# First channel mixer of a hybrid decoder trunk: from plain up projections to 17 folded pairs, and 32 modulation columns moved into the mLSTM heads

## The chip, the cores and the metric

The kernel runs on one core of a Trainium2 chip. The metric is the device time of one execution in microseconds (us). Times are medians of several executions; beside them stands one execution that was recorded by the hardware profiler, and every row of a profile comes from that one.

## What is computed

The trunk has two layers on a residual stream of 512 tokens by 1024 channels in float32. Layer 0 has a retention mixer, layer 1 an mLSTM mixer, and each layer then has a channel mixer (ConvFFN). Every mixer gets a normalised input, scaled and shifted by modulations that come from a vector c, and a third modulation (a gate) multiplies its output. Cut to what matters:

```python
def conv_ffn(h, w_up, conv_w, conv_b, w_down):
    u = causal_dwconv(h @ w_up, conv_w, conv_b)      # 1024 -> 2 x 2816, then 3 taps along the tokens
    a, b = jnp.split(u, 2, axis=-1)
    return (jax.nn.silu(a) * b) @ w_down             # 2816 -> 1024

c_act = jax.nn.silu(c)
for i in range(DEPTH):
    mod = c_act @ ada_w[i] + ada_b[i]
    sh_t, sc_t, gt_t, sh_f, sc_f, gt_f = [m[:, None, :] for m in jnp.split(mod, 6, axis=-1)]
    h = rmsnorm(x, norm_tok_g[i]) * (1.0 + sc_t) + sh_t
    y = retention_mixer(h, ...) if i % 2 == 0 else mlstm_mixer(h, ...)
    x = x + gt_t * y
    h = rmsnorm(x, norm_ffn_g[i]) * (1.0 + sc_f) + sh_f
    x = x + gt_f * conv_ffn(h, ffn_w_up[i], ffn_conv_w[i], ffn_conv_b[i], ffn_w_down[i])
return rmsnorm(x, final_g)
```

## The kernel before

**Layout.** Channels lie on the 128 partitions, tokens along the free axis: x is eight tiles of 128x512. A float32 product is made of three TensorE matmuls of parts of lower precision, high by high, high by low and low by high (`mm3`, L250 to L253). So each operand has a high and a low part, "hh" and "hl" for an input, "whi" and "wlo" for weights, "ggh" and "ggl" for the gated product that goes into the down projection.

**Weights** come in chunks of 512 KB (`Chunk`, L172): a load on the queue of SP into a raw buffer (a pool of eight, `RAWS`, which weights, modulation rows and the folding's buffers share), the high part as a cast on ScalarE (L157), the low part as a subtraction on VectorE (L162), into pools of eight (`WBUFS`).

**Modulations.** One column of 128 modulations is one instruction on VectorE over 128x1025 elements, with a sum (`gemv`, L134), on a row block `ada` of 512 KB that SP loads. Sixteen are taken at the very start; the other 80 stand in a list `side` (gates of layer 0's token mixer, 8; layer 0's channel mixer, 24; layer 1's token mixer, 24; layer 1's channel mixer, 24).

**Order of the work.** The kernel first builds a list `items`: each has the weight chunks that it uses, a function, and a flag `free`. A loop (from L1363) goes through them: it issues loads, high and low parts of chunks up to a few items ahead, though not past an item in `bars`, then calls the function, and then, behind an item that uses weights, is free and is not among the first, takes one entry off `side`. A scheduler then settles the order of each engine's instructions, by costs; inside a folded mixer's `run` the order is as written for TensorE, VectorE, ScalarE and GpSimd.

**The stages**: setup, retention heads, channel mixer 0, mLSTM heads, channel mixer 1, last normalisation. `heads` (L827) sets the order within the two token mixers: q and k, v, scores ("w", "sp", "sh", "sl": L1280 to L1284), gate, attention ("pav", "pden") of the four heads, with one head's parts between the next head's projections.

**Between stages** stand `boundary` (L580) and `Start`. `boundary` does the last contraction in two halves of the columns; under the second half the squares of the first are summed, its root is taken and normalised inputs are made. `Start` runs the first four projections of the next stage side by side ("pf" tiles), first for one half of the columns and then for the other, while the rest of the normalisation ends. With `folded=True` it keeps the normalised input "xr" too, and makes sums of it (`sums` and `turn`) which the folded products need, on VectorE, GpSimd and ScalarE.

**Channel mixer** (`Ffn`, L866). There are 22 pairs of up projections (one row block of the "a" half, one of the "b" half) and 22 row blocks of the down projection, in groups (`GROUPS`).
- Mixer 0 is *plain*. Each up projection ("pp" tiles, `proj_item`) is 24 matmuls of 512 columns; the convolution (L879, L884), silu, product and split follow on ScalarE and VectorE. The groups are 6, 8 and 8: the first two are contracted between projections ("po" tiles), the last in the boundary.
- Mixer 1 is *folded* from pair 5 on (`FOLD_FROM`). Pairs 0 and 1 are in `Start`, pairs 2 to 4 are six plain projections. Each of the other 17 pairs is a unit of `folded` (L374): instead of the eight half-size products of two projections it does seven products of combined weights and combined inputs, 12 matmuls of 256 columns each ("p" tiles, L387 to L389), and in between two pieces of the down projection, 12 matmuls of 512 columns each. `Fold` (L183) makes the combined weights of a pair from its two chunks "wa" and "wb": sums "ws" (L213, L214) and "wt" (L219, L220) on VectorE, high parts on ScalarE, low parts as a negated copy on ScalarE with an adding DMA on GpSimd's queue behind it (L165 to L170), or by a subtraction on VectorE. Unit 0's weights are prepared under the six plain projections, those of each later unit inside the unit before. The groups are 4, 4, 4, 4 and 6.

Of the kernel before, what the change touches and what calls it, by code (L numbers as in the profile page):

```python
# [22 lines left out]
FF = 2816  # L23
FT = FF // P
EPS = 1e-6
GROUPS = [[6, 8, 8], [4, 4, 4, 4, 6]]
WCOLS = 1024
WBUFS = 8
RAWS = 8
FOLD_FROM = 5  # L30
WPAD = 64
OFF = 16
# [37 lines left out]
def trunk(ctx: ExitStack, tc: tile.TileContext, xT, cb, pos, vec, decay, zmask, ada, w_s0, w_in0, w_v0,  # L70
# [4 lines left out]
    wpool = ctx.enter_context(tc.tile_pool(name="wpool", bufs=WBUFS))  # L75
    raws = ctx.enter_context(tc.tile_pool(name="raws", bufs=RAWS))
    cols = ctx.enter_context(tc.tile_pool(name="cols", bufs=4))
# [17 lines left out]
    def bank(s):  # L95
        return psum.tile([P, T], F32, tag="ps", name=uid(s))
# [75 lines left out]
    class Chunk:  # L172
        def __init__(self, src, n, off):
            self.raw, self.r, self.off = wide(uid("raw")), slice(0, n), off
            nc.sync.dma_start(self.raw[:, self.r], src)
# [74 lines left out]
    def mm3(o, ah, al, bh, bl, start, stop):  # L250
        PE.matmul(o, ah, bh, start=start, stop=False)  # L251
        PE.matmul(o, ah, bl, start=False, stop=False)  # L252
        PE.matmul(o, al, bh, start=False, stop=stop)  # L253
# [61 lines left out]
    items = []  # L315
# [7 lines left out]
    def item(uses, fn, free=True):  # L323
        for u in uses:
            if u.first is None:
                u.first = len(items)
            u.last = len(items)
        items.append((uses, fn, free))

    bars = []  # L330
    class Ahead:
# [5 lines left out]
        @property  # L337
        def flat(self):
            if not hasattr(self, "all"):
                self.all = [u for n, (uses, _, _) in enumerate(items) for u in uses if u.first == n]  # L340
            return self.all
# [19 lines left out]
    ahead = Ahead()  # L361

    side = []

    def proj_item(src, h, then):
        def fn(w):
            ps = bank("pp")
            for k in range(KT):
                cs = slice(k * P, k * P + P)
                mm3(ps[:], w[0].hi[:, cs], w[0].lo[:, cs], h[k].hi[:], h[k].lo[:], k == 0, k == KT - 1)  # L370
            then(ps)
        item([Use(src, KT * P)], fn)

    def folded(folds, h, terms, pairs, downs, ahead):  # L374
# [31 lines left out]
        def unit(i):  # L406
# [47 lines left out]
            if with_down:  # L454
                down(i, 0)
            else:
                product(i, 5, c1[:, HB])
# [9 lines left out]
            if d:  # L467
                d.high()
                d.low()
            down(i, 1)  # L470
            if f:
                f.high_b()
# [79 lines left out]
    def contract_tiles(w, n, gate, ys, i, t0, t1, after=lambda m: None, js=None):  # L552

        r = slice(t0, t1)
        per = WCOLS // (n * P)
        for j in js or range(per):
            m = i * per + j
            ps = bank("po")
            for k in range(n):
                cs = slice((j * n + k) * P, (j * n + k) * P + P)  # L560
                mm3(ps[:, r], w.hi[:, cs], w.lo[:, cs], ys(k).hi[:, r], ys(k).lo[:, r], k == 0, k == n - 1)
            add_residual(ps, m, gate(m), t0, t1)
            after(m)

    def pieces(src, n, gate, ys):

        per = WCOLS // (n * P)

        def piece(i):
            def run(w, t0, t1, after=lambda m: None, js=None):  # L570
                contract_tiles(w, n, gate, ys, i, t0, t1, after, js)
            return Use(src(i), per * n * P), run
        return [piece(i) for i in range(KT // per)]

    def contract_items(ps, between=lambda i: None):
        for i, (u, run) in enumerate(ps):
            item([u], lambda w, run=run: run(w[0], 0, T))
            between(i)

    def boundary(late, last, norm):  # L580


        for u, _ in late + last:
            u.off = OFF
        for p, after in ((0, lambda m: norm.square(0, m)), (1, norm.later)):
            for u, run in late:
                item([u], lambda w, run=run, p=p: run(w[0], *HALVES[p]), False)
                if p:
                    norm.beside()
            for u, run in last:  # L590
                item([u], lambda w, run=run, p=p, after=after: run(w[0], *HALVES[p], after), False)
        norm.rest()
# [268 lines left out]
    def gate_col(layer, which):  # L861
        base = (16, 40)[which]
        return lambda m: mods[layer][:, base + m : base + m + 1]


    class Ffn:  # L866
        def __init__(self, layer):
            self.layer, self.h, self.gs = layer, [], {}
            t0, t1 = self.pair(0), self.pair(1)
            w = w_up[layer]  # L870
            self.folded = layer == 1
            self.start = Start([w[0], w[FT], w[1], w[FT + 1]], self.h, layer, 1, [t0, t0, t1, t1], self.folded)

        def conv_col(self, f, j):
            return col("fcw", (self.layer * 3 + j) * 2 * FT + f)
# [62 lines left out]
                between()  # L938

        def down(self, gi):  # L940
            base = sum(GROUPS[self.layer][:gi])
            return pieces(lambda i: w_dn[self.layer][gi][i], GROUPS[self.layer][gi], gate_col(self.layer, 1),
                          lambda k: self.gs[base + k])

        def items(self, norm):
            groups = GROUPS[self.layer]
            if self.folded:
                w = w_up[self.layer]
                folds = [Fold((w[f], w[f + FT])) for f in range(FOLD_FROM, FT)]
                pairs = [self.steps(f) for f in range(FOLD_FROM, FT)]  # L950
                downs = [p for gi in range(len(groups) - 1) for p in self.down(gi)]
                steps, run = folded(folds, self.h, self.start.terms, pairs, downs, ahead)

                def early(n):
                    todo = [steps.pop(0) for _ in range(n)]
                    item([], lambda w: [f() for f in todo])
                self.up(2)
                early(1)
                self.up(3, lambda: early(3))
                th = self.pair(4)  # L960
                proj_item(w[4], self.h, th)
                early(len(steps))
                proj_item(w[4 + FT], self.h, lambda ps: (self.start.turn(), th(ps)))
                bars.append(len(items))
                item([], run)
                boundary([], self.down(len(groups) - 1), norm)
                return
            base, nxt = 0, 2
            for gi, n in enumerate(groups):
                upto = base + n + 2 if gi < len(groups) - 2 else FT  # L970
                while nxt < min(upto, FT):
                    self.up(nxt)
                    nxt += 1
                if gi < len(groups) - 1:
                    contract_items(self.down(gi))
                else:
                    boundary([], self.down(gi), norm)
                base += n


    cos, sin = slot("cos"), slot("sin")
# [372 lines left out]
    for which, layer in ((1, 0), (0, 1), (1, 1)):  # L1354
# [3 lines left out]
        base = (16, 40)[which]  # L1358
# [4 lines left out]
    for n, (uses, fn, free) in enumerate(items):  # L1363
        while ahead.at < len(ahead.flat) and ahead.may(n):
            ahead.load()
            ahead.high()
            ahead.low()
        fn([u.chunk for u in uses])
        if uses and free and n > 6 and side:
            side.pop(0)()  # L1370
    assert not side

# [1 line left out]
_ORDER = ["xT", "cb", "pos", "vec", "decay", "zmask", "ada", "w_s0", "w_in0", "w_v0", "w_o0", "w_in1", "w_v1",  # L1374
          "w_o1", "w_up"]
# [18 lines left out]
def _downs(w, groups):  # L1394
    got, at = [], 0
    for n in groups:
        per = WCOLS // (n * P)
        part = w[at * P : (at + n) * P].reshape(n, P, KT // per, per, P)
        got.append(part.transpose(2, 1, 3, 0, 4).reshape(KT // per, P, per * n * P))
        at += n  # L1400
    return got
# [74 lines left out]
```

## Time and profile before

| | us |
|---|---|
| median of 3 executions | 1569.84 (1569.71 to 1570.32) |
| the profiled execution | 1570.65 |
| its span, first to last instruction | 1568.8 |
| setup and retention heads | 0 to 416.7 |
| last half of their contraction, start of mixer 0 | 416.7 to 456.74 |
| mixer 0 from its fifth projection to the end of its contraction | 456.74 to 795.99 |
| start of the mLSTM mixer | 795.99 to 819.95 |
| mLSTM heads, their contraction and the start of mixer 1 | 819.95 to 1234.92 |
| mixer 1 from its fifth projection to the end of its contraction | 1234.92 to 1558.05 |
| end | 1558.05 to 1568.8 |

A row of the profile is one execution. Engines are PE (TensorE's matmuls), PEld (its weight loads), DVE (VectorE), ACT (ScalarE), POOL (GpSimd) and SP. A name such as `po<-ggh,whi` gives the tile that is written and those that are read; `x12` is a number of instructions. The duration of a matmul in a row overlaps with the next one, so the spacing is read from a window's length and its number of matmuls; a window counts two or three matmuls more that reach over its edges. In a timeline row the first two numbers are start and duration in us; in brackets stands the idle time of the engine before it and what ended it.

### The profile page before, as it was taken

How to read it: one execution, taken by the hardware profiler on the slowest of the kernel's cores; microseconds unless marked ns; L12 is line 12 of the kernel's file. 1: busy time of each engine (PE TensorE's matmuls, PEld its weight loads, DVE VectorE, ACT ScalarE, POOL GpSimd, SP SyncE). 2: the span in 40 equal slices, each digit the busy share in tenths (PEclk: the TensorE clock that was granted, in tenths of full speed). 3: DMA queues.
4: the chain of work that ended last, by engine and by line, in shares of the span. 5: the costliest groups of instructions: out<-in, count | busy, mean ns of one | idle time of the engine just before them, and what ended most of it. 6: DMA issues, size and time to landing. Idle time of an engine off the chain costs nothing. (4 is left out here: it accounts for less than half of the span.)

```text
span 1568.8 us, 21573 instructions
## 1 busy us (share of the span) xinstructions
PE 1539.3 (98%) x8428; PEld 1336.7 (85%) x8428; DVE 1136.2 (72%) x1631; ACT 772.1 (49%) x1142; POOL 186.2 (12%) x195
## 2 busy tenths in 40 slices
PE   7999999999999999999999999999999999999997
PEld 4788888888988888888998888888889889999997
DVE  7986678576979778764476667756588977777775
ACT  4534525353454334442356554555444666666763
POOL 3421010100200000000020011001022211111102
PEclk8999999999999999999999999999999999999999
DMA  8664365453236666533124322232312257767751
GB/s 297 223 198 135 101 228 181 162 181 119 97 97 197 225 207 188 174 102 99 55 86 133 105 74 75 94 107 68 107 54 74 76 132 203 175 189 187 184 140 54
DMA packets 66024, 219.14 MB, mean 140 GB/s; under 512 B 9073, under 2 KB 11377, under 8 KB 65922
## 3 DMA queue, kind: packets, MB, share of 16 engines
q1 hardware_dynamic: 59730, 195.22, 37.9%
q0 software_dynamic: 6192, 22.55, 7.7%
q8 instruction: 66, 1.08, 0.3%
q14 instruction: 36, 0.29, 0.1%
HBM read 193.06 MB, written 2.12 MB: 124 GB/s over the span
## 5 line engine op out<-in xcount | busy, mean ns | idle before, releaser
L162 DVE TENSOR_TENSOR wlo<-raw,whi 128x1024 fp32r<-128x1024 f32 (+1 forms) x224 | 271.5, 1214 | 135.2 <-ACT whi L157 133.8
L157 ACT CAST whi<-raw 128x1024 fp32r<-128x1024 f32 (+1 forms) x224 | 230.7, 1033 | 259.7 <-PE pp L252 95.9
L251 PE MATMUL pp<-hh,whi 128*128 128x512 f32 x832 | 323.9, 389 | 0.5 <-DVE vl L248 0.5
L252 PE MATMUL pp<-hl,whi 128*128 128x512 f32 x832 | 323.8, 389 | 0.0
L253 PE MATMUL pp<-hh,wlo 128*128 128x512 f32 x832 | 323.7, 389 | 0.0
L251 PEld LDWEIGHTS pp<-hh,whi 128*128 128x128 f32 x832 | 156.2, 188 | 33.4 <-DVE vl L248 1.0
L253 PEld LDWEIGHTS pp<-hh,wlo 128*128 128x128 f32 x832 | 156.2, 188 | 32.3
L252 PEld LDWEIGHTS pp<-hl,whi 128*128 128x128 f32 x832 | 156.2, 188 | 32.0
L550 DVE SCALAR_TENSOR_TENSOR x<-po,mod,x 128x512 f32<-128x512 f32 (+1 forms) x168 | 102.5, 618 | 95.8 <-PE po L253 95.7
L252 PE MATMUL po<-ggl,whi 128*128 128x512 f32 (+1 forms) x464 | 156.2, 337 | 0.0
L251 PE MATMUL po<-ggh,whi 128*128 128x512 f32 (+1 forms) x464 | 155.7, 337 | 0.1
L253 PE MATMUL po<-ggh,wlo 128*128 128x512 f32 (+1 forms) x464 | 155.8, 336 | 0.0
L252 PE MATMUL po<-yl,whi 128*128 128x256 f32 (+1 forms) x352 | 116.3, 330 | 0.0
L251 PE MATMUL po<-yh,whi 128*128 128x256 f32 (+1 forms) x352 | 116.2, 330 | 0.0
L253 PE MATMUL po<-yh,wlo 128*128 128x256 f32 (+1 forms) x352 | 116.2, 330 | 0.0
L134 DVE SCALAR_TENSOR_TENSOR ada<-ada,c_ext 128x1025 f32<-128x1025 f32 x93 | 114.9, 1239 | 0.0
L253 PEld LDWEIGHTS po<-ggh,wlo 128*128 128x128 f32 x464 | 87.1, 188 | 9.6
L251 PEld LDWEIGHTS po<-ggh,whi 128*128 128x128 f32 x464 | 87.1, 188 | 8.9 <-ACT ggh L913 0.3
L252 PEld LDWEIGHTS po<-ggl,whi 128*128 128x128 f32 x464 | 87.6, 189 | 8.2
L538 PE MATMUL pv<-wlo,hh 128*128 128x512 f32 x224 | 87.2, 389 | 0.0
L539 PE MATMUL pv<-whi,hl 128*128 128x512 f32 x224 | 87.0, 389 | 0.0
L537 PE MATMUL pv<-whi,hh 128*128 128x512 f32 x224 | 87.0, 389 | 0.0
(282 smaller groups left out, 3202.4 us busy)
## 6 DMA issues: line engine op xcount, KB each, us to landing
ada<-ada SPq DMA_DIRECT2D x96, 512.5 KB, 4.4
raw<-w_in SPq DMA_DIRECT2D x62, 512.0 KB, 3.4
raw<-w_up SPq DMA_DIRECT2D x54, 512.0 KB, 4.1
raw<-w_o SPq DMA_DIRECT2D x32, 512.0 KB, 3.3
raw<-w_dn SPq DMA_DIRECT2D x32, 512.0 KB, 4.4
raw<-w_v SPq DMA_DIRECT2D x28, 512.0 KB, 3.8
wb<-w_up SPq DMA_DIRECT2D x17, 512.0 KB, 3.8
wa<-w_up SPq DMA_DIRECT2D x17, 512.0 KB, 4.3
```

What stands on the lines that cost most here:

```text
L134: return V.scalar_tensor_tensor(raw, raw, 1.0, c_ext[:], op0=ALU.mult, op1=ALU.mult, accum_out=mods[layer][:, f : f + 1])
L157: A.copy(hi, w[:, r])
L162: V.tensor_tensor(lo, w[:, r], hi.bitcast(F32), op=ALU.subtract)
L251: PE.matmul(o, ah, bh, start=start, stop=False)
L252: PE.matmul(o, ah, bl, start=False, stop=False)
L253: PE.matmul(o, al, bh, start=False, stop=stop)
L537: PE.matmul(pss[t][:], h[k].hi[:, cs], w[0].hi[:, ws], start=st, stop=False)
L538: PE.matmul(pss[t][:], h[k].hi[:, cs], w[0].lo[:, ws], start=False, stop=False)
L539: PE.matmul(pss[t][:], h[k].lo[:, cs], w[0].hi[:, ws], start=False, stop=sp)
L550: V.scalar_tensor_tensor(x[m][:, r], ps[:, r], gate_col, x[m][:, r], op0=ALU.mult, op1=ALU.add)
```

## The change

Both channel mixers are built the same way: `Start` is always called with `folded=True`, `GROUPS` is one list for both, and the plain path of `items` is gone. So mixer 0 has 17 units of seven half-size products in written order, and its last group has 6 row blocks instead of 8. The list `side` is no longer emptied behind each item that allows it: up to the first bar (which stands ahead of mixer 0's units) entries are taken only until `LATER` = 32 are left. In the kernel before, all 80 were taken in retention and in the first items of mixer 0; now 44 are taken in retention as before, 4 under mixer 0's plain projections, and the last 32 (8 gates of layer 1's token mixer, 24 columns of its channel mixer) in the mLSTM heads, behind items of heads 0 to 2.

```diff
-GROUPS = [[6, 8, 8], [4, 4, 4, 4, 6]]
+GROUPS = [4, 4, 4, 4, 6]
...
+LATER = 32
...
-            self.folded = layer == 1
-            self.start = Start([w[0], w[FT], w[1], w[FT + 1]], self.h, layer, 1, [t0, t0, t1, t1], self.folded)
+            self.start = Start([w[0], w[FT], w[1], w[FT + 1]], self.h, layer, 1, [t0, t0, t1, t1], True)
...
         def items(self, norm):
-            groups = GROUPS[self.layer]
-            if self.folded:
-                w = w_up[self.layer]
-                folds = [Fold((w[f], w[f + FT])) for f in range(FOLD_FROM, FT)]
...
-                bars.append(len(items))
-                item([], run)
-                boundary([], self.down(len(groups) - 1), norm)
-                return
-            base, nxt = 0, 2
-            for gi, n in enumerate(groups):
-                upto = base + n + 2 if gi < len(groups) - 2 else FT
-                while nxt < min(upto, FT):
-                    self.up(nxt)
-                    nxt += 1
-                if gi < len(groups) - 1:
-                    contract_items(self.down(gi))
-                else:
-                    boundary([], self.down(gi), norm)
-                base += n
+            w = w_up[self.layer]
+            folds = [Fold((w[f], w[f + FT])) for f in range(FOLD_FROM, FT)]
+            pairs = [self.steps(f) for f in range(FOLD_FROM, FT)]
+            downs = [p for gi in range(len(GROUPS) - 1) for p in self.down(gi)]
+            steps, run = folded(folds, self.h, self.start.terms, pairs, downs, ahead)
+
+            def early(n):
+                todo = [steps.pop(0) for _ in range(n)]
+                item([], lambda w: [f() for f in todo])
+            self.up(2)
+            early(1)
+            self.up(3, lambda: early(3))
+            th = self.pair(4)
+            proj_item(w[4], self.h, th)
+            early(len(steps))
+            proj_item(w[4 + FT], self.h, lambda ps: (self.start.turn(), th(ps)))
+            bars.append(len(items))
+            item([], run)
+            boundary([], self.down(len(GROUPS) - 1), norm)
...
-        if uses and free and n > 6 and side:
+        if uses and free and n > 6 and side and (n > bars[0] or len(side) > LATER):
             side.pop(0)()
```

The lines of the new path are those of mixer 1's path before, one level further out.

More of the change, by code (lines that the diff above doesn't have):

```diff
@@ L940, in down @@
         def down(self, gi):
-            base = sum(GROUPS[self.layer][:gi])
-            return pieces(lambda i: w_dn[self.layer][gi][i], GROUPS[self.layer][gi], gate_col(self.layer, 1),
+            base = sum(GROUPS[:gi])
+            return pieces(lambda i: w_dn[self.layer][gi][i], GROUPS[gi], gate_col(self.layer, 1),
                           lambda k: self.gs[base + k])
         def items(self, norm):
-            groups = GROUPS[self.layer]
-            if self.folded:
-                w = w_up[self.layer]
-                folds = [Fold((w[f], w[f + FT])) for f in range(FOLD_FROM, FT)]
[L950 to L963, printed above, removed]
-                bars.append(len(items))
-                item([], run)
-                boundary([], self.down(len(groups) - 1), norm)
-                return
@@ L1463 @@
     for i in range(2):
-        for g, part in enumerate(_downs(a["ffn_w_down"][i], GROUPS[i])):
+        for g, part in enumerate(_downs(a["ffn_w_down"][i], GROUPS)):
             arrays[f"w_dn{i}{g}"] = c(part)
@@ L1471 @@
     with tile.TileContext(nc) as tc:
-        trunk(tc, *[args[n] for n in _ORDER], [[args[f"w_dn{i}{g}"] for g in range(len(GROUPS[i]))] for i in range(2)], out)
+        trunk(tc, *[args[n] for n in _ORDER], [[args[f"w_dn{i}{g}"] for g in range(len(GROUPS))] for i in range(2)], out)
     r = _run(nc, [arrays], core_ids=[0])
```

## The prediction

> **What bounds the kernel now.** I read the page's busy times and its forty slices first, then a table of windows cut at the stage borders of the trace.
>
> ```profile
> PE 1539.3 (98%) x8428; PEld 1336.7 (85%) x8428; DVE 1136.2 (72%) x1631; ACT 772.1 (49%) x1142; POOL 186.2 (12%) x195
> PE   7999999999999999999999999999999999999997
> DVE  7986678576979778764476667756588977777775
> PEclk8999999999999999999999999999999999999999
> ```
>
> TensorE works for 1539.3 of the 1568.8 us, in every slice but the ends, at full granted clock. So the time is the number of matmuls times their spacing, and a change gains what it takes from that product and loses every idle time that it opens. VectorE (72%) is the engine to watch: its slices reach 9, and it is in written order where the change puts work. The windows show the two mixers (columns: length, then busy time and count of PE, PEld, DVE, ACT, POOL, then granted clock, DMA share, GB/s):
>
> ```profile
> core 0: us, PE busy (x) PEld busy (x) DVE busy (x) ACT busy (x) POOL busy (x), PEclk, DMA share, GB/s
> 456.74:795.99 339.25, 339.25 (x1684) 288.79 (x1683) 238.34 (x329) 137.85 (x185) 8.71 (x8) 1.00 0.49 156
> 1234.92:1558.05 323.13, 323.01 (x2250) 301.30 (x2249) 240.81 (x369) 215.18 (x311) 43.23 (x51) 1.00 0.62 155
> 554.69:707.01 152.32, 152.32 (x674) 126.17 (x672) 110.63 (x148) 64.55 (x83) 0.00 (x0) 1.00 0.52 164
> 1288.76:1411.85 123.09, 123.09 (x866) 115.26 (x865) 94.09 (x141) 84.53 (x116) 17.22 (x20) 1.00 0.74 189
> ```
>
> The first two windows run from the first projection behind the four "pf" products to the last matmul of the down projection, for mixer 0 (plain) and mixer 1 (17 pairs folded): the same mathematics, both with TensorE idle for at most 0.12 us. The third holds 14 plain pairs, 672 matmuls of 512 columns: 152.32 / 672 = 226.7 ns each. The fourth holds eight folded units of 84 matmuls of 256 columns and 24 of 512: 15.39 us a unit.
>
> **A. What goes from TensorE's path.** A mixer 0 like mixer 1 takes 323.13 instead of 339.25 us: **−16.1 us**. As a check: a plain pair takes 48 x 0.2267 = 10.88 us; the seven products take 15.39 less the 24 down matmuls, 24 x 0.229 = 5.50, so 9.89 us, 117.8 ns each. 17 x 0.99 = 16.8; the wider spacing of the downs inside units (0.229) and the smaller last group nearly cancel. VectorE's 240.81 us and ScalarE's 215.18 would still fit beside 323. Bounds: −16.8 to −15.
>
> [...]
>
> **E. The start of mixer 0.** Folded, it also makes sums of the normalised input, on VectorE and GpSimd.
>
> ```profile
> 431.08:456.74 25.66, 23.14 (x196) 22.54 (x195) 16.41 (x30) 9.91 (x21) 4.26 (x5) 1.00 0.20 63
> 1208.26:1234.92 26.66, 23.71 (x196) 23.07 (x195) 25.87 (x47) 10.98 (x24) 7.74 (x9) 1.00 0.11 40
> ```
>
> The plain start of mixer 0 is 25.66 us, the folded one of mixer 1 26.66, with VectorE at 25.87 of it. Part of those 25.87 are sums of unit 0's weights, which the built order of the changed mixer 0 puts later (B). Between 0 and +1.0: **+0.5**.
>
> **B. The way into unit 0.** Six plain projections separate the start from the units; under them unit 0's weights are folded, and in mixer 0 four of the modulations that stay are also taken.
>
> ```profile
> 1234.92:1267.59 32.67, 32.67 (x146) 27.05 (x145) 27.69 (x44) 24.87 (x37) 2.78 (x3) 1.00 0.49 129
> 1214.12 0.68 DVE L213 TENSOR_TENSOR ws<-wb 128x512 f32<-128x512 f32 x1
> 1228.50 0.68 DVE L219 TENSOR_TENSOR wt<-wa,wt 128x512 f32<-128x512 f32 x1
> 474.21 1.22 DVE L134 SCALAR_TENSOR_TENSOR ada<-ada,c_ext 128x1025 f32<-128x1025 f32 x1
> 475.35 0.74 DVE L884 SCALAR_TENSOR_TENSOR cv<-pp,vecs,cv 128x510 f32<-128x510 f32 x1
> wlo<-wt POOLq DMA_DIRECT2D x9, 512.0 KB, 5.0
> ```
>
> In mixer 1 VectorE is busy for 27.69 of these 32.67 us, and the first and last sum of unit 0's weights (1214.12, 1228.50) lie before them. In the changed mixer 0 the four sums (4 x 0.68 = 2.7) fall inside, and four modulations: 1.14 us each from its start to the next instruction (474.21 to 475.35), 4.6. 27.7 + 2.7 + 4.6 = 35.0 us in 32.67: 2.3 us too many, if VectorE never waits. Behind the last sum stands the low part of that pair on GpSimd's queue, 5.0 us to landing, which product 6 needs, and the input sums' low parts, which unit 0 needs. I take **+3.3** of idle (0, if ScalarE and the DMA overlap better, to 6, the overrun and most of the 5.0). An idle of that length has a second price:
>
> ```profile
> 40.20:44.00 3.80, 3.80 (x10) 3.03 (x11) 3.73 (x5) 0.63 (x3) 3.63 (x3) 0.59 0.51 165
> 40.19 0.50 PE L1143 MATMUL pst<-whi,hl 128*128 128x512 f32 x1 [1.82 <-DVE hl L308]
> 53.95 0.50 PE L1141 MATMUL pst<-whi,hh 128*128 128x512 f32 x1 [2.75 <-ACT hh L306]
> 54.00:58.00 4.00, 3.89 (x10) 2.82 (x11) 4.00 (x9) 1.77 (x3) 0.00 (x0) 0.57 0.84 247
> 809.07 0.39 PE L252 MATMUL pf<-hl,whi 128*128 128x256 f32 x1 [1.29 <-DVE hl L308]
> ```
>
> After idles of 1.82 and 2.75 us the granted clock is 0.59 and 0.57 for some 4 us, which costs 4 x 0.42 = **+1.7**; after 1.29 us (809.07) the clock stays 1.00. By these rows B is **+5.0** in all. [...]
>
> **C. The start of the second mixer pair.** The last down group has 6 instead of 8 rows of weights, so a column half lasts 144 matmuls instead of 192, while VectorE's adds, squares, root and normalisation under it stay.
>
> ```profile
> 779.03:795.99 16.96, 16.96 (x146) 16.96 (x145) 15.61 (x22) 12.72 (x21) 7.24 (x6) 1.00 0.52 166
> 795.99:819.95 23.96, 22.66 (x196) 22.47 (x195) 14.53 (x25) 9.01 (x18) 3.38 (x4) 1.00 0.18 60
> 1193.89:1208.26 14.37, 14.37 (x124) 14.37 (x123) 13.69 (x20) 9.81 (x17) 5.83 (x6) 1.00 0.23 76
> ```
>
> Now 16.96 us lie between the first root and the end of the contraction, with VectorE at 15.61; the start behind it takes 23.96. Ahead of mixer 1 those are 14.37 us (13.69), and the start took 26.66, ahead of mixer 0 25.66. The changed kernel comes into that class: +1.7 to +2.7 by these, 0 if the work spreads. **+2.0**.
>
> **D. The mLSTM heads.** 32 modulations go from mixer 0, whose units are gapless without them, into heads 0 to 2. Each brings a 512 KB load on SP's queue into a buffer of the pool of eight that it shares with the weights: 16.8 MB in some 211 us are 80 GB/s on top of 95, less than the 189 of the units, so the loads themselves hide; but a modulation that VectorE takes late holds a weight's buffer.
>
> ```profile
> 820.00:1031.00 211.00, 210.28 (x969) 175.32 (x968) 146.71 (x189) 113.73 (x161) 16.82 (x18) 1.00 0.32 95
> 903.00:961.00 58.00, 57.28 (x272) 47.77 (x272) 40.30 (x56) 31.52 (x48) 8.26 (x9) 1.00 0.25 74
> 210.00:260.00 50.00, 50.00 (x229) 41.79 (x229) 42.79 (x59) 20.40 (x31) 7.90 (x10) 1.00 0.55 176
> 887.40 1.28 ACT L1283 ACT_TABLE_LOAD   x1 [0.96 <-DMA mb<-scratch]
> 887.42 0.35 DVE L1280 SCALAR_TENSOR_TENSOR w<-mb,bcols,zm 128x128 f32<-128x128 f32 x1 [0.26 <-DMA mb<-scratch]
> 894.55 1.05 ACT L157 CAST whi<-raw 128x1024 fp32r<-128x1024 f32 x1 [1.63 <-PE pp L252]
> 894.58 0.39 PE L251 MATMUL pav<-sh,vh 128*128 128x512 f32 x1
> 895.63 1.22 DVE L162 TENSOR_TENSOR wlo<-raw,whi 128x1024 fp32r<-128x1024 f32 x1 [2.12 <-ACT whi L157]
> 900.91 0.39 DVE L248 TENSOR_TENSOR sl<-sp,sh 128x128 fp32r<-128x128 f32 x1 [0.37 <-ACT sh L247]
> 903.07 0.40 PE L256 MATMUL pden<-sumsh,ones 128*128 128x512 f32 x1
> ```
>
> VectorE is busy for 146.7 of those 211 us; 32 x 1.14 = 36.5 and some gains bring it to 87%, what the retention heads carry at 42.79 of 50 without idling TensorE. In the mean it fits. The order is what costs. Now head 0's score chain begins at 887.40, and a weight chunk's cast, which waits for TensorE's last "pp" to free its buffer (894.55), and its low part (895.63) stand in the middle of that chain. In the built order of the changed kernel that chunk's cast and low part stand ahead of the chain's table load and first "w". So the chain starts after 895.6 + the low part's 1.2 = 896.8 instead of 887.4, while TensorE reaches "pav" at 894.58. Behind it come the table load, exp, w and sp, sh (as 887.40 to some 891 now), which overlap the low part in part: first "pav" at about 899.1, **4.5 us of idle**. The chain now takes 13.5 us to its last "sl" (900.91) with 3.4 of them spent on that chunk; without it the last sl is late by 5 to 6 and "pden" (903.07), behind 1.8 of slack, by about 4. Queued behind the chunk's low part on VectorE are the chain, the next head's conv and the modulations; the next products wait for nothing else. The 0.72 us that TensorE idles in 903 to 961 I leave as they are. **+4.0**, from 0 to 17 (below).
>
> **Sum**: −16.1 + 0.5 + 5.0 + 2.0 + 4.0 = **−4.6 us**. The profiled execution took 1570.65 (span 1568.8 and 1.85 around it), 0.81 above the median of 1569.84; so 1566.05 beside it, and **1565.2** as a median.
>
> **Rivals.** (1) *Slower: the heads' chain is caught behind a weight chunk three times.* The modulations in heads 0, 1 and 2 push VectorE back each time, so that a chunk that waits for TensorE stands ahead of each score chain: 4.5 of idle and 1.7 of clock, three times 18.6 in place of 4.0: −4.6 + 14.6 = +10, **1580**. It decides when the heads lose over 11.8 us (8.7, plus 3.1 for 0.2%). For it: 87% of VectorE in written order, and the built order of head 0. Against: retention at 86% has no idle.
>
> (2) *Nothing gained: two places.* Head 0's chain costs its clock spell too (6.2) and head 1's mean or value chain another 3: D = 9, **1570**.
>
> [...]
>
> (4) *All is hidden.* ScalarE, DMA and VectorE overlap as in retention, and only E stays: −15.6, **1554**. Against: the chunk ahead of the chain is in the built order, and VectorE's overrun under the six projections is arithmetic.
>
> **How the numbers follow.** Chances: forecast 0.37 (own range 1560 to 1570), rival 1 0.20, rival 2 0.18, rival 3 0.10, rival 4 0.15. A measurement of this kernel tells about 0.2%, 3.1 us, from no change. Faster: 0.31 of the forecast, all of rivals 3 and 4, −0.01 for spread: 0.55. Same: 0.06 of the forecast and most of rival 2: 0.23. Slower: rival 1 and the top of rival 2: 0.22. The range of 8 in 10 is 1556 to 1577: it leaves out half of rival 4 and rather more than half of rival 1.
>
> **What would show it.** A right: mixer 0's units at 15.39 us each without idle. B: an idle of TensorE at unit 0's products 5 to 6 and a stretch at 0.57 to 0.6 clock behind it. C: the start behind mixer 0 at 25.7 to 26.7 us. D: "pav" of head 0 released by ScalarE or VectorE after some 4.5 us. Wrong: units longer than 15.4 us (A), or idle before the products of the first projections or the values in heads 1 and 2 (rival 1).

## The result, and the profile after

The changed kernel takes 1584.79 us (1584.16 to 1585.62 in 4 runs) against 1570.08 us before in the same comparison: a ratio of 1.0094, interval 1.0077 to 1.0112. It is slower by 14.7 us, where 4.6 us less were forecast, and lies above the range.

The page of the changed kernel, busy times and two of the forty-slice rows:

```profile
span 1582.3 us, 23062 instructions
PE 1531.8 (97%) x8992; PEld 1352.1 (85%) x8992; DVE 1201.9 (76%) x1782; ACT 859.1 (54%) x1282; POOL 227.3 (14%) x242
PE   7999999999998999999999899999999999999997
DVE  7986678676987777777877688866578977777775
```

TensorE's busy time fell by 7.5 us (1539.3 to 1531.8) while the span grew by 13.5: it idles 50.5 us instead of 29.5. Two slices that were full are not full any more, the 13th (mixer 0's entry) and the 23rd (head 0 of the mLSTM). The same stages as before, in windows of the changed kernel:

```profile
430.40:456.13 25.73, 23.43 (x196) 22.64 (x195) 23.82 (x43) 10.93 (x25) 7.76 (x9) 1.00 0.20 63
456.13:787.95 331.82, 325.54 (x2248) 302.72 (x2247) 253.97 (x387) 220.84 (x317) 45.09 (x51) 0.99 0.68 173
787.95:814.58 26.63, 23.37 (x197) 22.67 (x195) 18.62 (x32) 10.90 (x23) 3.39 (x4) 1.00 0.25 83
814.58:1221.84 407.26, 394.03 (x1925) 332.36 (x1923) 301.93 (x427) 199.77 (x294) 42.37 (x44) 0.98 0.40 127
1248.49:1571.56 323.07, 322.96 (x2250) 301.24 (x2249) 240.71 (x369) 215.34 (x311) 43.08 (x51) 1.00 0.62 155
510.44:571.98 61.54, 61.54 (x433) 57.63 (x432) 46.98 (x71) 42.29 (x58) 8.60 (x10) 1.00 0.76 184
```

And the heads before, in one window:

```profile
819.95:1208.26 388.31, 387.59 (x1924) 329.54 (x1923) 263.74 (x354) 198.87 (x294) 40.31 (x44) 1.00 0.29 89
```

| stage | before | after | difference | forecast |
|---|---|---|---|---|
| setup and retention, to the first "pf" of mixer 0 | 431.08 | 430.40 | −0.7 | 0 |
| start of mixer 0 (E) | 25.66 | 25.73 | +0.1 | +0.5 |
| mixer 0 (A and B) | 339.25 | 331.82 | −7.4 | −11.1 |
| start of the mLSTM (C) | 23.96 | 26.63 | +2.7 | +2.0 |
| mLSTM heads (D) | 388.31 | 407.26 | +18.95 | +4.0 |
| the rest | 360.54 | 360.46 | −0.1 | 0 |

The sum is 13.5. Mixer 0's units run as mixer 1's did: four of them in 61.54 us, 15.385 each, without idle (the row from 510.44). Against mixer 1's 323.1 the whole mixer 0 is 8.7 us longer, all at its entry. Of the heads' 18.95 us, 12.5 are idle of TensorE (13.23 against 0.72) and 6.4 are the same matmuls at a lower clock (394.03 busy against 387.59). The idle times of TensorE of over 0.9 us in these two stages, in the timeline:

```profile
497.15 0.43 PE L388 MATMUL p<-t24h,whi 128*128 128x256 f32 x1 [2.15 <-ACT fs L425]
500.65 0.58 PE L390 MATMUL p<-t24h,wlo 128*128 128x256 f32 x1 [2.86 <-DMA wlo<-wt]
896.38 0.79 PE L252 MATMUL pav<-sh,vh 128*128 128x512 f32 x1 [6.76 <-ACT sh L248]
937.36 0.54 PE L252 MATMUL pp<-hh,whi 128*128 128x512 f32 x1 [1.12 <-DVE vl L249]
969.66 0.50 PE L257 MATMUL pden<-sumsh,ones 128*128 128x512 f32 x1 [0.94 <-ACT o L1280]
1043.51 0.80 PE L252 MATMUL pp<-hh,whi 128*128 128x512 f32 x1 [3.03 <-DVE vl L249]
```

The first two are unit 0, the others heads 0, 1 and 2. The granted clock (third number from the end) is low behind four of them, as the rows show, and 0.54 behind 500.65 too; behind 969.66 it stays 1.00:

```profile
497.00:501.00 4.00, 0.99 (x3) 0.69 (x4) 2.18 (x4) 3.04 (x4) 0.85 (x1) 0.54 0.81 221
896.38:900.40 4.02, 4.02 (x9) 2.48 (x10) 2.74 (x5) 1.77 (x5) 1.01 (x1) 0.53 0.45 178
937.00:941.00 4.00, 3.64 (x9) 2.93 (x10) 3.78 (x7) 0.94 (x1) 0.00 (x0) 0.58 0.86 225
1043.50:1047.50 4.00, 3.99 (x11) 3.19 (x12) 2.09 (x4) 1.35 (x2) 0.00 (x0) 0.57 0.79 221
```

Head 0, in the timeline of the changed kernel, ScalarE and VectorE:

```profile
891.37 1.04 ACT L158 CAST whi<-raw 128x1024 fp32r<-128x1024 f32 x1 [0.65 <-DMA raw<-w_in]
891.98 1.22 DVE L135 SCALAR_TENSOR_TENSOR ada<-ada,c_ext 128x1025 f32<-128x1025 f32 x1
892.43 1.28 ACT L1269 ACT_TABLE_LOAD   x1
893.12 1.22 DVE L163 TENSOR_TENSOR wlo<-raw,whi 128x1024 fp32r<-128x1024 f32 x1
894.26 0.35 DVE L1266 SCALAR_TENSOR_TENSOR w<-mb,bcols,zm 128x128 f32<-128x128 f32 x1
```

That is the order that the prediction read off: a weight chunk's cast, then the table load; a modulation and the chunk's low part, then the first "w", 4.6 us behind the last "pp" of TensorE (889.6). Only the releaser differs: here the cast waited last for the chunk's load (0.65 us), not for TensorE. Head 2 is another case; the window ahead of its "pp", after and before:

```profile
1022.00:1045.00 23.00, 19.97 (x93) 16.75 (x92) 21.56 (x27) 12.22 (x18) 0.00 (x0) 0.97 0.54 178
```

```profile
1011.00:1036.00 25.00, 25.00 (x119) 21.12 (x118) 17.46 (x21) 11.84 (x17) 0.00 (x0) 1.00 0.32 106
```

VectorE is busy for 21.56 of 23 us, before for 17.46 of 25: convolutions, low parts, head 1's root and two modulations stand in line, and the low parts of the values ("vl") that let "pp" go come 3.03 us late.

### The profile page after: what moved, and what is told of

It is laid out like the page before. It is cut to its first block, busy times and chain, and to the rows that moved or that the text cites. A ratio compares the mean times of both kernels' runs of the same rounds, so it can differ in the third digit from the quotient of the medians.

```text
span 1582.3 us, 23062 instructions
## 1 busy us (share of the span) xinstructions
PE 1531.8 (97%) x8992; PEld 1352.1 (85%) x8992; DVE 1201.9 (76%) x1782; ACT 859.1 (54%) x1282; POOL 227.3 (14%) x242
## 4 chain that ended last, share of the span: by engine, by line
PE 75%; DVE 15%; ACT 4%; DMA 3%; issue 2%; POOL 0%; SPq 0%; DVEq 0%; ACTq 0%; POOLq 0%
PE po L252 8%; PE po L253 8%; PE po L254 8%; PE p L390 7%; PE p L388 7%; PE p L389 7%; PE pp L252 6%; PE pp L253 6%; PE pp L254 6%; DVE wlo L163 3%; PE pv L539 2%; PE pv L538 2%; PE pv L540 2%; DVE ada L135 2%; DVE hl L309 1%
## 5 line engine op out<-in xcount | busy, mean ns | idle before, releaser
L252 PE MATMUL pp<-hh,whi 128*128 128x512 f32 x560 | 219.5, 392 | 4.2 <-DVE vl L249 4.2
L253 PE MATMUL pp<-hl,whi 128*128 128x512 f32 x560 | 219.3, 392 | 0.0
L254 PE MATMUL pp<-hh,wlo 128*128 128x512 f32 x560 | 219.0, 391 | 0.0
L388 PE MATMUL p<-hh,whi 128*128 128x256 f32 x544 | 152.9, 281 | 0.6 <-ACT hh L248 0.6
L389 PE MATMUL p<-hl,whi 128*128 128x256 f32 x544 | 152.9, 281 | 0.6 <-DVE hl L249 0.6
L390 PE MATMUL p<-hh,wlo 128*128 128x256 f32 x544 | 152.9, 281 | 0.0
L254 PEld LDWEIGHTS pp<-hh,wlo 128*128 128x128 f32 x560 | 105.9, 189 | 22.1
L253 PEld LDWEIGHTS pp<-hl,whi 128*128 128x128 f32 x560 | 105.8, 189 | 21.9
L879 ACT ACTIVATE cv<-p,vecs 128x512 f32<-128x512 f32 x68 | 53.0, 780 | 114.4 <-PE p L390 76.2
L389 PEld LDWEIGHTS p<-hl,whi 128*128 128x128 f32 x544 | 104.4, 192 | 0.8 <-DVE hl L249 0.8
L388 PEld LDWEIGHTS p<-hh,whi 128*128 128x128 f32 x544 | 102.1, 188 | 0.9 <-ACT hh L248 0.8
```

What stands on the lines that cost most here:

```text
L388: PE.matmul(o, hi[:, ch], b[0], start=st, stop=False, skip_group_check=True)
L389: PE.matmul(o, hi[:, ch], b[1], start=False, stop=False, skip_group_check=True)
L390: PE.matmul(o, lo[:, cl], b[0], start=False, stop=sp, skip_group_check=True)
L879: A.activation(acc[:], ps[:], AF.Identity, bias=col("fcb", self.layer * 2 * FT + f), scale=self.conv_col(f, 2))
```

## The experiments

Two theories of the heads: (1) the columns' instructions on VectorE, in its fixed order, delay the chains that TensorE waits for; (2) the columns' rows take every second buffer of the shared pool, so weights load late. The waits of SP's queue spoke for (2) (changed kernel, 814 to 1045 us; columns: what was waited for, us in total, times, longest):

```profile
SPq L176 <- DVE ada L135: 76.9, 24, 17.1
SPq L176 <- DVE wlo L163: 42.7, 15, 5.7
```

In 24 waits of 76.9 us in all, a weight load on SP stood waiting for a modulation to release a row's buffer. Long waits are nothing new to this queue, though: in the kernel before its weight loads wait 180.2 us for low parts (820 to 1031 us), and TensorE idles 0.72 us there.

**The heads alone.** The kernel before, its mixer 0 plain, with only the 32 columns moved:

```diff
+    ml_at = len(items)                      # behind mixer 0's items
-        if uses and free and n > 6 and side:
+        if uses and free and n > 6 and side and (n >= ml_at or len(side) > 32):
```

> The kernel before with its plain channel mixer 0, and only the last 32 modulation columns moved into the mLSTM heads. Theory 1 (the columns' instructions on VectorE push the heads' chains) and theory 2 (the columns' rows take weight buffers, so the heads' weights arrive late) both put the loss in the heads and independent of the folding: the heads grow by 18.9 us as in the changed kernel, the time is about 1589. If the heads lose because of the folded stage ahead of them instead, the time stays at 1570.

Measured: 1588.8 us, ratio 1.0119 (1.0089 to 1.0148).

```profile
820.79:1226.90 406.11, 392.75 (x1924) 332.33 (x1923) 301.87 (x427) 199.73 (x294) 42.34 (x44) 0.98 0.39 127
```

The heads take 406.1 us, 17.8 more than before, behind a plain mixer 0. So the loss belongs to the move, not to the folding.

**Rows or instructions.** In the changed kernel, for the last 32 columns, with a `variant` that does (a) nothing, (b) the load alone, (c) VectorE's work alone, on c:

```diff
     def side_gemv(layer, f):
+        if len(side) < LATER:
+            variant(layer, f)
+            return
         tc.keep_in_program_order(gemv(layer, f))
```

(a) 

> The changed kernel without its last 32 columns: rows not loaded, instructions not issued (the 32 modulations stay zero, so layer 1's gates and its channel mixer's scale and shift are left out). Both theories: the heads' 18.9 us go, about 1566, with the 9 us of unit 0's entry and the 2.7 us of the mLSTM start still there. If those three stages hang together, less than 1562.

(b) 

> The changed kernel with the 32 rows loaded into the shared buffers but no instruction on VectorE that reads them (the same 32 modulations are left out). Theory 1: as without the columns, about 1566. Theory 2: the rows still take every second buffer and SP's queue, though a buffer is free as soon as the row has landed: 1570 to 1585.

(c) 

> The changed kernel with VectorE's work for the 32 columns but no rows: two instructions of 512 elements each on c, resident, in place of one of 1025 (the 32 modulations are wrong values, their rows left out). Theory 1: the loss stays, 1580 to 1585. Theory 2: weights load as without the columns, about 1566.

Measured: (a) 1568.73 us, ratio 0.9990 (0.9979 to 1.0001); (b) 1570.72, 1.0001 (0.9990 to 1.0013); (c) 1591.75, 1.0137 (1.0108 to 1.0167). The heads, one window each:

```profile
818.89:1207.18 388.29, 387.57 (x1925) 329.50 (x1923) 263.77 (x354) 198.93 (x294) 40.39 (x44) 1.00 0.27 89
```

```profile
819.12:1208.62 389.50, 388.19 (x1925) 329.35 (x1924) 265.07 (x354) 199.08 (x294) 40.66 (x44) 1.00 0.36 121
```

```profile
814.94:1227.91 412.97, 394.62 (x1924) 333.57 (x1923) 304.35 (x491) 200.32 (x294) 40.46 (x44) 0.98 0.26 85
```

Without columns the heads are as before (388.29), with the rows alone 1.2 us longer, with the instructions alone 24.7 us longer. (b) prices the loads and their bytes, not the waits: with no instruction to read a row, its buffer is free when the row has landed, and no load waits for a modulation. What decides is (c): without a row no load can wait for one, and the whole loss is there, with idles of 5.64, 4.02 and 7.58 us in heads 0, 1 and 2. So theory (1) is enough for the loss. Whether the 76.9 us of waits add to it in the change itself is not shown; at head 0 the late load holds the cast for 0.65 us. (c) is longer than the change, perhaps because two short instructions take more of VectorE than one long (304.35 us in the heads against 301.93). On VectorE, head 0's first "w" stands ahead of the weight chunk's low part in (a) and (b), and behind it in (c), as in the change.

**The entry of unit 0.** First theory, B1: one weight load on SP waits 39.5 us, from mixer 0's start to 475.95, for the first of the four columns to release its row's buffer, and unit 0's weights are prepared late behind it. Rival, B2: VectorE's instructions themselves.

```profile
SPq L176 <- DVE ada L135: 39.5, 1, 39.5
```

The four columns taken earlier, two behind each of four retention items:

```diff
+TWICE = (56, 57, 58, 59)
...
             side.pop(0)()
+            if n in TWICE:
+                side.pop(0)()
```

> The changed kernel with the four columns that it takes under mixer 0's six plain projections taken in the retention heads instead (two behind each of four items). Theory B1 (a column's row holds a buffer for 39.5 us, the weight load behind it on SP's queue waits, so unit 0's combined weights are prepared late): the 6.2 us of idle and the slow clock at unit 0 go, mixer 0 takes 323 to 325 instead of 331.8, the time is 1576 to 1578. Theory B2 (VectorE's instructions alone are too many): 4.6 us of them go, mixer 0 about 327, 1580. If neither, 1585.

Measured: 1579.85 us, ratio 1.0058 (1.0036 to 1.0080); mixer 0 takes 325.42 us, 6.4 less. That removes the wait and the instructions together, so it settles nothing between B1 and B2. Two more, with the same edit as (b) and (c) above but for the four columns:

> The changed kernel, whose four columns under mixer 0's six plain projections keep their work on VectorE (two instructions of 512 elements on c, resident) but load no rows (these four modulations are wrong values). Theory B1 (a row holds its buffer, SP's queue waits 39.5 us for it, unit 0's weights load late): the entry loses 1 to 3 us instead of 8.7, mixer 0 takes 324 to 326. Theory B2 (VectorE's instructions are too many): mixer 0 stays at 330 to 332.

> The changed kernel whose four columns under the six projections load their rows, but nothing on VectorE reads them (these four modulations stay zero). A buffer is free once its row has landed, so SP's queue does not wait for VectorE. Both theories: mixer 0 at 324 to 327. If it stays at 330 to 332, neither the wait nor the instructions are the cause, but the rows' bytes.

Measured: 1586.90 us (1.0103, 1.0074 to 1.0132) with the instructions, 1581.28 (1.0065, 1.0043 to 1.0088) with the rows. Mixer 0:

```profile
457.00:788.95 331.95, 326.29 (x2249) 303.51 (x2247) 253.15 (x392) 220.57 (x317) 45.04 (x51) 0.99 0.67 170
```

```profile
460.06:785.16 325.10, 323.46 (x2248) 301.80 (x2247) 247.91 (x375) 220.46 (x317) 45.03 (x51) 1.00 0.68 174
```

With the instructions and no row the whole loss stays (331.95), with the rows and no instruction it is gone (325.10), although SP's queue waits 24.9 and 22.1 us for other things there. So B2 alone is enough for the loss. That B1 cost nothing is not shown: the issue of the low part of unit 0's "wt", in the change and in the run with instructions alone, is

```profile
490.92 0.85 POOL L170 DMA_DIRECT2D wlo<-wt  x1 [6.74 <-ACT wlo L169]
473.86 0.85 POOL L177 DMA_DIRECT2D wlo<-wt  x1 [3.81 <-ACT wlo L176]
```

Behind the wait for the row it comes 17 us later, and TensorE's last idle in unit 0 of the change (2.86 us) is for it. Without the row that idle does not occur, but the one ahead of it, at "fs", is 4.46 us instead of 2.15; two of the four columns stand later in VectorE's order there, at 489.21 and 494.98 us. The loss has two ways into unit 0, and these runs do not tell what the wait would cost without the instructions.

**Density or place in the heads.** The 32 columns over all four heads, behind 32 of some 55 items, alone and with the four early ones:

```diff
+    late = [n for n, (uses, _, free) in enumerate(items) if uses and free and n > bars[0] and n < bars[1] - 12]
+    late = {late[len(late) * i // LATER] for i in range(LATER)}
...
-        if uses and free and n > 6 and side and (n > bars[0] or len(side) > LATER):
+        if uses and free and n > 6 and side and (n in late or n <= bars[0] and len(side) > LATER):
```

> The changed kernel with the same 32 columns in the mLSTM heads, but behind 32 of some 55 items, evenly over all four heads, instead of behind the first 32. Theory 1 (VectorE's instructions, too dense in heads 0 to 2): the heads lose 2 to 6 instead of 18.9, the time 1568 to 1572. If the order of the score chain costs by itself, whatever the density: 1578 or more.

> Both edits at once: four columns in retention and 32 spread over the mLSTM heads. If the stages add up, the sum of the two gains: 1560 to 1564, faster than the kernel before by 6 to 10 us; if spreading does not help, 1575 or more.

Measured: 1577.13 us (1.0046, 1.0031 to 1.0061) and 1570.51 (1.0003, 0.9994 to 1.0013); both above what was expected of a cure by density alone. The heads of the first:

```profile
814.73:1214.66 399.93, 392.02 (x1924) 331.20 (x1923) 300.36 (x427) 199.82 (x294) 40.99 (x44) 0.99 0.40 129
```

Still 11.6 us over before: spreading took 7.3 of the 18.95. Head 0 idles 4.41 us, and its order still has the chunk ahead of "w". So the next also leaves out the items of q and k of heads 0 and 1:

```diff
+    late = late[:5] + late[13:]
```

> As the last experiment (four columns in retention, 32 spread over the mLSTM heads), but none behind the eight projections of heads 0 and 1's q and k, so that in the built order head 0's first w stands ahead of the weight chunk again. If that place in the order is what idles head 0, the 4.4 us before pav and the slow clock behind it go: the heads lose 3 to 7 instead of 12 us, the time is 1562 to 1566. If VectorE's amount of work is enough by itself: 1570.

Measured: 1568.51 us, 0.9992 (0.9982 to 1.0003), between the two cases that were expected. The built order is restored, and head 0's idle is 0.60 us instead of 4.41. The heads take 396.02 us; the largest idle is now in head 2, in the second row:

```profile
809.58:1205.60 396.02, 390.05 (x1924) 330.73 (x1923) 303.33 (x427) 200.08 (x294) 41.78 (x44) 1.00 0.40 131
1005.00:1031.00 26.00, 22.59 (x102) 18.77 (x101) 23.62 (x35) 12.00 (x17) 0.00 (x0) 0.95 0.54 183
```

VectorE is busy for 23.62 of 26 us there, with three columns ahead of "vl", and TensorE idles 3.41. Restoring the place took another 3.9 us by these windows; the 7.7 that stay are put down to VectorE's amount of work where the columns are dense, which this run alone does not show. One profiled execution of each is a coarse measure for this step: ten executions of this version lie between 1564.17 and 1572.89 us, and the medians with and without the restored order differ by 2.0.

**Another engine.** Columns in the heads on GpSimd and ScalarE:

```diff
+            G.tensor_tensor(raw, raw, c_ext[:], op=ALU.mult)
+            A.activation(raw, raw, AF.Copy, accum_out=mods[layer][:, f : f + 1])
```

> Four columns in retention, and the 32 of the mLSTM heads (at the changed kernel's places) as a product on GpSimd and a sum on ScalarE instead of one instruction on VectorE. If it is VectorE's instructions that cost: the heads lose 2 to 8 instead of 18.9 us, 1562 to 1568. If GpSimd holds each row's buffer longer (2.7 us for one product in the setup) and ScalarE stands in the score chain too: 1575 or more.

Measured: 1610.55 us, 1.0259 (1.0242 to 1.0275), the worst of all. GpSimd's group of the products, in the lines of that run:

```profile
L147 POOL TENSOR_TENSOR ada<-ada,c_ext 128x1025 f32<-128x1025 f32 x32 | 82.4, 2580 | 98.9 <-DMA ada<-ada 68.1 <-issue 13.4 <-DVE z L821 6.1
```

Each holds GpSimd for 2.58 us. The trace shows where this reaches TensorE, on ScalarE, whose sums wait in its order for these products:

```profile
891.22 1.06 ACT L148 ACTIVATE ada<-ada 128x1025 f32<-128x1025 f32 x1 [4.78 <-POOL ada L147]
```

Behind this sum stands the cast "mqkh" (892.92), for which TensorE idles 7.06 us. From 860 to 1010 us ScalarE waits 38.3 us for GpSimd's products, and TensorE's three longest waits there (12.5, 10.1 and 6.6 us in all) are for ScalarE. So the run does not price VectorE's work on another engine as such, but a chain of two engines in their fixed orders.

**The columns in the units.** Seventeen columns inside mixer 0's units, 15 spread over the heads behind head 1's k, the four in retention:

```diff
         def unit(i):
+            col = row(None)                 # mixer 0 only: loads the row of one column
...
             product(i, 3, c1[:, HB])
+            row(col)                        # its instruction on VectorE
...
-LATER = 32
+LATER = 15
+    late = late[13:]
```

> Four columns in retention, 17 of the 32 in mixer 0's units, one at the end of each, written into their order, and 15 spread over the mLSTM heads behind q and k of head 1. In a unit VectorE is busy for 11.8 of 15.4 us and a column takes 1.15: if the units hide it, mixer 0 stays at 325 to 327, the heads lose 1 to 4, the time is 1558 to 1562. If the row's buffer delays the units' weights, each unit grows by 0.3 to 1 us: 1566 to 1578.

Measured: 1560.78 us, 0.9945 (0.9927 to 0.9963), faster than both. Four units, then mixer 0 and the heads:

```profile
510.44:571.98 61.54, 61.54 (x435) 57.63 (x434) 51.58 (x79) 42.27 (x59) 8.59 (x10) 1.00 0.84 224
456.82:781.63 324.81, 322.82 (x2249) 300.99 (x2247) 270.14 (x415) 221.20 (x317) 45.04 (x51) 1.00 0.75 203
808.25:1197.97 389.72, 388.27 (x1925) 329.46 (x1923) 285.64 (x392) 199.94 (x294) 41.79 (x44) 1.00 0.34 110
```

The units stay at 15.385 us with a column in each: VectorE goes from 46.98 to 51.58 of 61.54, all of it hidden. With 15 columns in the heads instead of 32 these take 389.72, 1.4 us over before, which agrees with density as the cause of the 7.7 us above.

**The last down group.** Mixer 0's groups as 4, 4, 3, 3 and 8, in the changed kernel and in the last one:

```diff
-GROUPS = [4, 4, 4, 4, 6]
+GROUPS = [[4, 4, 3, 3, 8], [4, 4, 4, 4, 6]]
```

> The changed kernel with mixer 0's down groups of 4, 4, 3, 3 and 8 instead of 4, 4, 4, 4 and 6, so that the last contraction is as long as in the kernel before. If the shorter half is what makes the mLSTM start 2.7 us longer, that start returns from 26.6 to some 24.0 and the time is 1582; if the start's length comes from something else, it stays at 26.6 and 1584.8.

> The kernel with 17 columns in the units, four in retention and 15 spread over the later heads, with mixer 0's down groups of 4, 4, 3, 3 and 8. If the stages add up: 1560.8 less 2.6, 1558; if the shorter units (18 down matmuls in place of 24) no longer hide VectorE's work with a column in each, 1561 or more.

Measured: 1583.73 us (1.0088, 1.0068 to 1.0108) and 1558.78 (0.9928, 0.9911 to 0.9945). The mLSTM start, in the one and in the other:

```profile
791.15:815.51 24.36, 23.06 (x196) 22.87 (x195) 14.47 (x25) 9.05 (x19) 3.39 (x4) 1.00 0.18 61
```

```profile
783.06:807.02 23.96, 22.67 (x196) 22.48 (x195) 14.47 (x25) 9.00 (x18) 3.38 (x4) 1.00 0.17 60
```

With a last group of 8 the start is back at 24.4 and 23.96 us: the shorter half is what made it longer. In the changed kernel the whole gains only 1.1 us of the 2.7 that were expected, less than its two executions differ (1581.98 and 1585.49). 1558.78 us is the best version found, 0.7% below the kernel before.

## Why the prediction was wrong

**A was right.** −16.1 us was read from mixer 1, and mixer 0's units came out at the same 15.385 us; with the entry mended mixer 0 takes 325.1 to 325.4 us.

**E** (+0.5) was +0.1, and **C** (+2.0) +2.7, with the mechanism that it named, shown by the last two runs.

**B had the mechanism right and the size wrong.** +5.0 was 8.7, 6.2 of idle and the rest clock. That VectorE's instructions are enough for it is what the run with instructions and no rows shows. The 2.3 us too many held "if VectorE never waits"; it was busy for 29.31 of the 32.67 us from 456.13, so of the 35.0 that were counted some 5.7 were left over, an estimate from these rows. The sum also counted one idle; in the change TensorE waits four times, at "hh", "hl", "fs" and the low part of "wt" (0.59, 0.57, 2.15 and 2.86 us). The last, issued late behind the wait for the row, took 9.7 us from issue to landing instead of 5.0; beside it ran unit 1's loads, with the DMA engines at 0.81 to 0.93, but why it took longer was not tried.

**D is the step that failed.** "In the mean it fits", at 87%, and only head 0's order was priced, at 4.0. Measured: 18.95. Three things were missing. Head 0's idle was 6.76, not 4.5: the cast of the chunk ahead of the chain began 1.75 us behind the last "pp" instead of at once, behind two other casts of ScalarE and 0.65 us of waiting for its own load, and a modulation (891.98) stood ahead of its low part. Its clock spell was left out, although B had priced one by the same rows: 6.4 us of the 18.95 are slow clock. And heads 1 and 2 were taken to be free: ahead of head 2's "pp" VectorE is busy for 21.56 of 23 us, and what TensorE waits for lies behind it. Retention, the row taken as a proof that 86% is harmless, was an average, and no evidence on a chain; why retention carries it was not tried.

**Rival 1** was the case: three heads caught, at 18.6 us, measured 18.95. Its mechanism was half right: a chunk ahead of the chain in head 0, but VectorE's queue ahead of "vl" in heads 1 and 2. That 18.6 and 18.95 are so close is luck: it counted three equal idles of 4.5 us, and the runs show 6.76, 1.12, 0.94 and 3.03 and some smaller ones. Its total, 1580, was short by B's 3.7 and C's 0.7. It had a chance of 0.20, and rather more than half of it was outside the range. Rival 2 named two things that did come, head 0's clock spell and a late value chain in head 1, but its 9 us for D were half of what was measured. Rival 3, a clock that holds at unit 0, and rival 4 fall: the clock did drop there, to 0.54, and neither unit 0's entry nor the heads were hidden.

## What to carry to other kernels

Where TensorE has no idle, work moved to another stage is priced at the chains in that stage that end last, over stretches of some 20 us and in the built order of the engine, not at the engine's mean; each stall found is then priced with its clock spell (here 0.53 to 0.58 over some 4 us behind five of the six idles in the timeline, 1.00 behind the sixth). A long wait of a queue need not be the cause of a loss: run the rows and the instructions apart before believing it, and ask of each such run which waits it takes away besides. A stage that is written out by hand and whose VectorE has 3 us free in each 15 was the better place for the moved work, which took it without a trace.

## What the runs showed of the hardware that had not been expected

The clock does not follow from the length of the idle alone. At the same place, product 6 of unit 0, TensorE idles 1.99 us with early columns (up to 495.51). With spread ones besides it idles no longer: mixer 0's idle is 2.10 us in all in both (325.42 less 323.32 busy, 327.03 less 324.93). The 4 us behind it, in the first and in the second:

```profile
495.50:499.50 4.00, 3.99 (x23) 3.58 (x24) 2.04 (x4) 3.97 (x5) 0.86 (x1) 1.00 0.10 20
```

```profile
495.74:499.74 4.00, 4.00 (x18) 3.52 (x19) 2.03 (x4) 3.97 (x5) 0.85 (x1) 0.68 0.10 20
```

In the first the granted clock stays 1.00, in the second it is 0.68, and mixer 0 is 1.6 us longer (327.03 against 325.42). With the last down group of 8 besides the columns in the units it idles 1.65 us there (up to 496.54), and the clock stays 1.00. In the kernel before it fell after 1.82 us, to 0.59 (40.19). Nor is the last idle alone the measure: in the change it fell to 0.58 after 1.12 us (937.36), with another 0.64 us of idle and two matmuls just ahead. Executions of one version differ too: the two with early columns took 1577.14 us at a mean clock of 0.990, the one of the row, and 1582.56 at 0.987. What decides between a clock that stays and one that falls was not shown.
